# One DMA ring in a fixed order with 8-row tiles, in place of two rings with 6-row tiles, for silu(x1)*x2

## The chip, the cores and the metric

The kernel runs on one core of a Trainium2 chip. Times are device microseconds of a whole execution.

"Engine" means two things below. VectorE, ScalarE and SyncE are the core's instruction engines. A "DMA engine" is one of the 16 that move bytes. A "ring" is the queue of transfers that one issuing engine fills: SyncE's shows as q1, ScalarE's as q10.

## The reference

```python
batch, seq, dim = (32, 512, 2048)            # float32
x1, x2 = x[..., :1024], x[..., 1024:]
out = x1 * (1 / (1 + np.exp(-x1))) * x2      # [32, 512, 1024]
```

There are 16,384 rows: 134.2 MB in, 67.1 MB out, and little arithmetic for each byte.

## The kernel before

128 partitions each take a run of consecutive rows: tiles of 4 rows per partition, twenty times 6, and 4 again. Loads are issued by SyncE, stores by ScalarE, so the two directions sit in two rings.

```python
in_pool  = ctx.enter_context(tc.tile_pool(name="in_pool", bufs=2))
out_pool = ctx.enter_context(tc.tile_pool(name="out_pool", bufs=4))
# plan = [4] + [6]*20 + [4] rows per partition; KC = 2
for bi, (row0, K) in enumerate(plan):
    xv = x_flat[row0:row0 + P * K].rearrange("(p k) d -> p k d", k=K)
    ov = out_flat[row0:row0 + P * K].rearrange("(p k) d -> p k d", k=K)
    xt = in_pool.tile([P, KT, in_cols], dt, name="xt")
    nc.sync.dma_start(out=xt[:, :K, :], in_=xv)              # load, SyncE's ring
    ot = out_pool.tile([P, KT, half], dt, name="ot")
    for c in range(0, K, KC):
        ce = min(c + KC, K)
        nc.scalar.activation(out=ot[:, c:ce, :], in_=xt[:, c:ce, :half], func=Silu)
        nc.vector.tensor_mul(out=ot[:, c:ce, :], in0=ot[:, c:ce, :], in1=xt[:, c:ce, half:])
    nc.scalar.dma_start(out=ov, in_=ot[:, :K, :])            # store, ScalarE's ring
# (names shortened, asserts cut)
```

## Time and profile before

The time before is 474.58 us, the median of three runs (474.44 to 474.65).

| | before |
|---|---|
| span of the profile | 473.1 us |
| bytes moved | 201.35 MB, 426 GB/s over the span |
| DMA share and rate from 36 to 459 us | 1.00, 433 GB/s |
| VectorE, ScalarE busy | 30%, 25% |

The page of the kernel before: busy time of the two compute engines, the DMA row in 40 slices (tenths of the 16 DMA engines' time), and the two rings with packets, MB and share of the 16 engines' span.

```profile
span 473.1 us, 296 instructions
DVE 142.9 (30%) x64; ACT 118.9 (25%) x65; POOL 0.2 (0%) x4
DMA  8999999999999999999999999999999999999995
q1 hardware_dynamic: 3168, 134.22, 65.9%
q10 hardware_dynamic: 3168, 67.11, 33.0%
```

The DMA row is full until its last digit. The compute engines are idle most of the time and only wait for loads. The last digit, 5, is the one visible weakness. The windows view of the same kernel opens it up. Its columns are the stretch, its length, busy time of each engine with its instructions in brackets, the TensorE clock, the DMA share and GB/s.

```profile
core 0: us, DVE busy (x) ACT busy (x) POOL busy (x), PEclk, DMA share, GB/s
36.00:459.00 423.00, 130.55 (x59) 104.88 (x58) 0.00 (x0) 1.00 1.00 433
463.50:466.50 3.00, 2.22 (x2) 0.00 (x0) 0.00 (x0) 1.00 0.00 0
```

The timeline of the kernel before from 459 us on (start, length, engine, line, operation; in brackets the idle time before it and what ended that):

```profile
459.29 3.71 ACT L64 ACTIVATE ot<-xt 128x2048 f32<-128x2048 f32 x2 [10.47 <-DMA xt<-in_x_dram]
461.23 4.49 DVE L69 TENSOR_TENSOR ot<-ot,xt 128x2048 f32<-128x2048 f32 x2 [9.29 <-ACT ot L64]
465.76 0.34 ACTq L74 DMA_DIRECT2D out_dram<-ot  x1
```

The last load has landed at 459.3 us. Both chunks must be computed before the one store is issued at 465.8 us, and the other stores run out at about 463.5 us: 3.0 us in which no byte moves.

### The profile page before, as it was taken

The page shows a single profiled execution, that of the slowest core. Times are in us where ns is not written, and L with a number is a line of the kernel's source. Part 1 is how long each engine was busy: PE and PEld are TensorE (multiplying, and loading weights), DVE is VectorE, ACT ScalarE, POOL GpSimd, SP SyncE. Part 2 cuts the span into 40 slices and gives each one's busy share as a digit, 9 for nine tenths or more (in the row PEclk, how much of TensorE's full clock was granted, in tenths as well). Part 3 has the DMA queues.
Part 4 walks back from the last instruction along what each step waited for, and adds up shares of the span by engine and source line. Part 5 has one row for each costly group of instructions (what it writes and reads, how often), then busy time and mean ns, then how long its engine had stood idle before and what let it go on. Part 6 is the DMA issues. An engine that isn't in the chain of part 4 may idle for free.

```text
span 473.1 us, 296 instructions
## 1 busy us (share of the span) xinstructions
DVE 142.9 (30%) x64; ACT 118.9 (25%) x65; POOL 0.2 (0%) x4
## 2 busy tenths in 40 slices
DVE  0323505050514324050505142231505050513323
ACT  1340404041231404040413214040404042231411
POOL 0000000000000000000000000000000000000000
DMA  8999999999999999999999999999999999999995
GB/s 355 449 398 424 432 430 455 420 428 451 414 432 441 432 443 432 416 434 447 426 428 457 418 435 436 443 432 424 432 443 418 438 453 411 451 432 418 433 420 244
DMA packets 6338, 201.35 MB, mean 426 GB/s; under 512 B 704, under 2 KB 704, under 8 KB 704
## 3 DMA queue, kind: packets, MB, share of 16 engines
q1 hardware_dynamic: 3168, 134.22, 65.9%
q10 hardware_dynamic: 3168, 67.11, 33.0%
q14 instruction: 2, 0.02, 0.0%
HBM read 134.22 MB, written 67.11 MB: 426 GB/s over the span
## 4 chain that ended last, share of the span: by engine, by line
DMA 78%; DVE 14%; ACT 4%; issue 1%; DVEq 0%; SPq 0%; ACTq 0%
DMA xt<-in_x_dram 78%; DVE ot L69 14%; ACT ot L64 4%; DVEq L100 0%; SPq L59 0%; ACTq L64 0%
## 5 line engine op out<-in xcount | busy, mean ns | idle before, releaser
L69 DVE TENSOR_TENSOR ot<-ot,xt 128x2048 f32<-128x2048 f32 x64 | 142.9, 2287 | 322.8 <-ACT ot L64 322.8
L64 ACT ACTIVATE ot<-xt 128x2048 f32<-128x2048 f32 x64 | 117.6, 1899 | 343.4 <-DMA xt<-in_x_dram 343.4
L64 ACT ACT_TABLE_LOAD x1 | 1.3, 1283 | 0.7 <-PEq L89 0.7
L89 POOL MEMSET const-bfloat16-1.0<- 128x1 bf16 x1 | 0.1, 103 | 0.0
L89 POOL MEMSET const-uint8-127<- 128x1 uint8 x1 | 0.1, 103 | 0.0
L89 POOL MEMSET const-float32-1.0<- 128x1 f32 x1 | 0.1, 100 | 0.0
L89 POOL MEMSET const-float32-0.0<- 128x1 f32 x1 | 0.1, 99 | 0.2 <-issue 0.2
## 6 DMA issues: line engine op xcount, KB each, us to landing
xt<-in_x_dram SPq DMA_DIRECT2D x20, 6144.0 KB, 34.8
out_dram<-ot ACTq DMA_DIRECT2D x20, 3072.0 KB, 27.8
xt<-in_x_dram SPq DMA_DIRECT2D x2, 4096.0 KB, 20.7
out_dram<-ot ACTq DMA_DIRECT2D x2, 2048.0 KB, 15.4
```

The costliest lines, as they stand in the source:

```text
L64: nc.scalar.activation(out=ot[:, c:ce, :], in_=xt[:, c:ce, :half], func=mybir.ActivationFunctionType.Silu,)
L69: nc.vector.tensor_mul(out=ot[:, c:ce, :], in0=ot[:, c:ce, :], in1=xt[:, c:ce, half:],)
L89: nc = _bacc.Bacc("TRN2", target_bir_lowering=False, num_devices=1)
```

## The change

Its intent: fewer and longer runs in HBM (64 KiB loads, 32 KiB stores), a fixed order of load and store in one ring so that the two directions do not mix, store issues off ScalarE's queue, and a last store in four pieces so that the first bytes leave sooner.

```diff
-    K_MAIN = 6
-    K_EDGE = 4
+    K = 8
     KC = 2
-    out_pool = ctx.enter_context(tc.tile_pool(name="out_pool", bufs=4))
+    out_pool = ctx.enter_context(tc.tile_pool(name="out_pool", bufs=2))
     ... (plan of tiles cut)
+    def load(i):
+        xt = in_pool.tile([P, K, in_cols], dt, name="xt")
+        nc.sync.dma_start(out=xt, in_=xv[i])
+        loaded[i] = xt
+    load(0)
+    load(1)
+    for i in range(n_tiles):
+        xt = loaded.pop(i)
+        last = i == n_tiles - 1
     ... (activation and multiply by chunks of 2 rows, unchanged)
-        nc.scalar.dma_start(out=ov, in_=ot[:, :K, :])
+            if last:
+                nc.sync.dma_start(out=ov[i][:, c:ce, :], in_=ot[:, c:ce, :])
+        if not last:
+            nc.sync.dma_start(out=ov[i], in_=ot)
+        if i + 2 < n_tiles:
+            load(i + 2)
```

The ring then holds L0 L1 S0 L2 S1 L3 ... S13 L15 S14 and the four pieces of S15. Below, "L5" and "S5" are the load and the store of tile 5.

More of the change, by code (lines that the diff above doesn't have):

```diff
@@ L24 @@
     dt = x_flat.dtype
-    K_MAIN = 6
-    K_EDGE = 4
+    K = 8
     KC = 2
+    n_tiles = num_rows // (P * K)
+    assert n_tiles * P * K == num_rows
     in_pool = ctx.enter_context(tc.tile_pool(name="in_pool", bufs=2))
-    out_pool = ctx.enter_context(tc.tile_pool(name="out_pool", bufs=4))
-    rows_per_part_total = num_rows // P
-    rem = rows_per_part_total - 2 * K_EDGE
-    if rem > 0 and rem % K_MAIN == 0:
-        plan_k = [K_EDGE] + [K_MAIN] * (rem // K_MAIN) + [K_EDGE]
-    else:
-        plan_k = []
-        rem = rows_per_part_total
-        while rem > 0:
-            k = min(K_MAIN, rem)
-            plan_k.append(k)
-            rem -= k
-    plan = []
-    row = 0
-    for k in plan_k:
-        plan.append((row, k))
-        row += P * k
-    assert row == num_rows
-    KT = max(K_MAIN, K_EDGE)
-    for bi, (row0, K) in enumerate(plan):
-        xv = x_flat[row0:row0 + P * K].rearrange("(p k) d -> p k d", k=K)
-        ov = out_flat[row0:row0 + P * K].rearrange("(p k) d -> p k d", k=K)
-        xt = in_pool.tile([P, KT, in_cols], dt, name="xt")
-        nc.sync.dma_start(out=xt[:, :K, :], in_=xv)
-        ot = out_pool.tile([P, KT, half], dt, name="ot")
+    out_pool = ctx.enter_context(tc.tile_pool(name="out_pool", bufs=2))
+    xv = x_flat.rearrange("(n p k) d -> n p k d", p=P, k=K)
+    ov = out_flat.rearrange("(n p k) d -> n p k d", p=P, k=K)
+    loaded = {}
+    def load(i):
[7 more added lines that the diff above has]
+        last = i == n_tiles - 1
+        ot = out_pool.tile([P, K, half], dt, name="ot")
         for c in range(0, K, KC):
-            ce = min(c + KC, K)
+            ce = c + KC
             nc.scalar.activation(
```

## The prediction

In the text below, the 463 us are an estimate, worked out from the port ceiling that it cites.

> **What bounds the kernel now.** The 16 DMA engines. On the profile's page VectorE is busy 30% of the span and ScalarE 25%, while the DMA row reads 9 in nearly every slice. From 36 to 460 us the windows view gives a DMA share of 1.00 at 433 GB/s. The Trainium skill ("DMA: Bandwidth & Descriptors", Where 436 GB/s comes from) puts the port ceiling at 435 GB/s; the trace agrees within half a per cent. The job moves 201.3 MB whatever the tiling, at 435 GB/s 463 us of the 473.1 us span. About 10 us is to win.
>
> **Where those 10 us are** (the trace's packet records of before):
> - about 2.0 us at the start, before all engines carry data;
> - a hole at the end: packets run out at about 463.5 us and start again at 466.6 us (window 463 to 467: DMA share 0.18). The last load landed at 459.3 us; two activations and two multiplies must finish (465.7 us) before the one last store is issued. About 3.0 us;
> - about 1.5 us from the last data packet to the end;
> - a fixed cost per packet: 49,152 B take 1815 ns, 24,576 B 912 ns, so about 9 ns are fixed, the rest runs at 27.2 B/ns; 352 data packets per engine cost about 3.2 us;
> - about 1.8 us of slow first packets.
>
> **What the change does.**
> 1. Last store in four pieces, the store of tile 14 queued right behind the last load. Estimate from the trace: activation 1.9, multiply 2.29 us, so pieces are ready about 4.2, 6.5, 8.8 and 11.1 us after the last load lands, plus about 1.3 us issue. The store before them keeps the engines busy for 9.7 us, each piece 2.4 us. The last piece is ready before its turn (17 us), so the hole closes: -3.0 us, on the critical path.
> 2. Fewer, longer packets: 128 x 64 KiB, 120 x 32 KiB and 32 x 8 KiB per engine, 280 instead of 352: -0.65 us. If a 64 KiB run is cut in two, about +0.5 us instead.
> 3. One ring instead of two: nothing. Load-only (2 to 20 us) and store-only (459 to 463 us) stretches of before run packets at the same durations as the mixed ones; no gap shows between the first two loads. The queue must not run dry: compute of a tile takes about 11 us, the load still queued behind it 19.3 us, so the next store and load are issued in time though the one queue waits in order.
> 4. Store issues leave ScalarE (22 x 0.36 us): off the critical path.
>
> Sum: 474.6 - 3.0 - 0.6 = 471.0 us, 0.8% faster. Range 469.3 to 473.6. Faster by over 2%: 1%; within 2%: 94%; slower by over 2%: 5%.
>
> **What would show it right.** The DMA row full until the last slice, no hole before the last store; all data on one queue, about 5,040 packets (about 7,090 if 64 KiB runs are cut); steady rate about 433 GB/s; 64 KiB packets at about 2417 ns.
>
> **What would make it wrong.** Gaps at the 30 switches between store and load in one ring: this pattern is not in the trace of before; 0.3 us each would be +9 us, three times the gain. Or a 64 KiB stride between partitions in HBM that slows reads (packets above 2430 ns; 32 and 48 KiB show no such thing). Or the ring running dry, seen as DMA gaps ended by a VectorE wait on SP.

## The result, and the profile after

The changed kernel took 476.43 us (median of 4 runs, 475.81 to 476.81), against 474.55 us for the kernel before in the same rounds. The ratio is 1.0037, with a 95% interval of 1.0022 to 1.0051. A ratio is the mean time of one kernel's runs over that of the other's in the same rounds, so it is not quite the ratio of the medians. The change costs 0.4% instead of saving 0.8%. The predicted range was 469.3 to 473.6 us.

The page of the changed kernel:

```profile
span 474.4 us, 266 instructions
DVE 142.4 (30%) x64; ACT 118.2 (25%) x65; POOL 0.2 (0%) x4
DMA  8999999999999999999999999999999999989996
DMA packets 5042, 201.35 MB, mean 424 GB/s; under 512 B 560, under 2 KB 560, under 8 KB 560
q1 hardware_dynamic: 5040, 201.33, 98.8%
```

Much of what was predicted is there. One ring carries everything, with exactly 5,040 packets, so 64 KiB runs are not cut in two. The DMA row is full and shows no dry ring. The windows of the changed kernel:

```profile
core 0: us, DVE busy (x) ACT busy (x) POOL busy (x), PEclk, DMA share, GB/s
36.00:448.00 412.00, 124.57 (x56) 102.33 (x56) 0.00 (x0) 1.00 1.00 432
459.50:469.20 9.70, 5.43 (x3) 1.90 (x2) 0.00 (x0) 1.00 1.01 420
469.60:473.10 3.50, 0.00 (x0) 0.00 (x0) 0.00 (x0) 1.00 0.19 80
```

The last line is the surprise. From 469.6 to 473.1 us the DMA engines are not idle and not busy, but at 0.19: three or four of the sixteen still work and the others have finished. And the timeline of the changed kernel at its end:

```profile
454.09 7.31 ACT L56 ACTIVATE ot<-xt 128x2048 f32<-128x2048 f32 x4 [21.64 <-DMA xt<-in_x_dram]
456.03 8.90 DVE L61 TENSOR_TENSOR ot<-ot,xt 128x2048 f32<-128x2048 f32 x4 [20.05 <-ACT ot L56]
458.35 6.94 SPq L67 DMA_DIRECT2D out_dram<-ot  x4
```

The last load lands at 454.0 us.

### Looking at single DMA engines

The views above average over the 16 DMA engines, so I went to the trace's packet records (start, duration, bytes, ring of each packet). They do not name their engine. But a busy engine starts a packet within a few ns of the end of the one before, so the records can be sorted into 16 sequences. Where two engines' packets end together, sequences can be swapped by mistake; a jump by a whole packet is such an artefact or can be one, and I do not use it. A tile's load is eight packets per engine. "Lag" is the end of the eighth packet on an engine minus the median of the 16.

The lag in ns of the four latest engines at every second load of the changed kernel, worked out from these records (the other twelve stay within about 0.5 us of the median):

```
load          L1    L3    L5    L7    L9   L11   L13   L15
engine a     418   635  1587  2372  3360  3996  4365  4845
engine b     486   786  2087  2746  3662  3865  4415  4702
engine c     240   264   462  1248  2041  2701  3393  3719
engine d     137   205   249   557  1309  1839  2533  3005
```

In the kernel before, about five engines are late too, by 0.8 to 1.6 us after L2. But they keep that lag to the ns over most of the execution. In the changed kernel lag grows, tile by tile.

Where does it grow? A 65,536 B packet takes 2418 ns nearly always (predicted: 2417). From 60 us on, 45 of the 224 load packets that are directly followed by a store are stretched by more than 60 ns, up to 988 ns. Of the 1,505 that are followed by another load, 2 are. Of 208 store packets followed by a load, none is. So the loss is at one place: the last packet of a load before a store, on engines that are late already. Of the 45, 40 are on the four engines of the table; the other five are stretched by at most 0.13 us. In this kernel it is the last packet alone: on these engines 11 second-last load packets also ran for more than 1 us after the median engine had gone over to its store, and none is stretched.

How this becomes time: 12 engines run out of packets at 469.2 to 469.3 us and the last one at 473.2 us, 3.9 us. The lag also delays the landing of the last load, because a load has landed when its last DMA engine is done. The median engine finishes it at 448.8 us, the last at 453.7 us. So the first piece of the last store is issued late, at 458.35 us, and twelve engines idle 0.2 to 1.1 us at 459 us before it. The 3.9 us and about 1 us together account for the 4.9 us from the span that the prediction amounts to (473.1 less 3.6, 469.5 us) to the measured 474.4 us.

### The profile page after: what moved, and what is told of

The parts are those of the page before. It is cut to its first block, busy times and chain, and to the rows that moved or that the text cites. A ratio compares the mean times of both kernels' runs of the same rounds, so it can differ in the third digit from the quotient of the medians.

```text
span 474.4 us, 266 instructions
## 1 busy us (share of the span) xinstructions
DVE 142.4 (30%) x64; ACT 118.2 (25%) x65; POOL 0.2 (0%) x4
## 3 DMA queue, kind: packets, MB, share of 16 engines
q1 hardware_dynamic: 5040, 201.33, 98.8%
## 4 chain that ended last, share of the span: by engine, by line
DMA 79%; DVE 15%; ACT 3%; SPq 1%; DVEq 0%; issue 0%; ACTq 0%
DMA xt<-in_x_dram 79%; DVE ot L61 15%; ACT ot L56 3%; SPq L69 1%; DVEq L97 0%; SPq L45 0%; ACTq L56 0%
```

## The experiments

Theory A: sharing one ring makes late DMA engines later at each switch from load to store, and the slowest engine sets the time. Rival B: 64 KiB packets, or their stride in HBM, do it. Fifteen kernels ran.

### 1. two_rings_k8: the change without its one ring

```diff
-                nc.sync.dma_start(out=ov[i][:, c:ce, :], in_=ot[:, c:ce, :])
+                nc.scalar.dma_start(out=ov[i][:, c:ce, :], in_=ot[:, c:ce, :])
-            nc.sync.dma_start(out=ov[i], in_=ot)
+            nc.scalar.dma_start(out=ov[i], in_=ot)
```

> The changed kernel with its stores moved back to ScalarE's ring; tiles of 8 rows and the four-piece last store stay. Theory A (on one ring, the last load packet before a store is stretched on the engines that run late, 0.1 to 1.0 us each time, and their lag grows tile by tile to 4.8 us): lag stays constant as in the kernel before (0 to 1.6 us), no stretched packets after the first store, time about 471 to 472 us. Rival B (64 KiB load packets or their stride cause it): lag grows as in the changed kernel, about 476 us.

Measured: 471.95 us (471.85 to 472.20, 4 runs), ratio to the kernel before 0.9941 (0.9926 to 0.9956). The latest engine's lag is 0.48 us at L1, still 0.48 us at L10, and at most 0.75 us at L15. Of 1,504 load packets followed by a store packet, 2 are stretched. The page of this kernel, then its windows:

```profile
span 470.1 us, 267 instructions
q1 hardware_dynamic: 2304, 134.22, 66.3%
q10 hardware_dynamic: 2736, 67.11, 33.1%
```

```profile
36.00:448.00 412.00, 124.55 (x56) 102.32 (x56) 0.00 (x0) 1.00 1.01 434
464.50:466.00 1.50, 0.78 (x1) 0.00 (x0) 0.00 (x0) 1.00 0.52 218
468.70:470.10 1.40, 0.00 (x0) 0.00 (x0) 0.00 (x0) 1.00 0.00 0
```

The same 5,040 packets, on two rings, end together: all 16 engines stop between 468.7 and 468.8 us. Only the ring differs from the changed kernel, so the one ring costs 4.5 us (476.43 less 471.95). B falls.

### 2. one_ring_k6: the one ring with the old tiles

```diff
-        nc.scalar.dma_start(out=ov, in_=ot[:, :K, :])
+            if last:
+                nc.sync.dma_start(out=ov[:, c:ce, :], in_=ot[:, c:ce, :])
+        if not last:
+            nc.sync.dma_start(out=ov, in_=ot[:, :K, :])
+        if i + 2 < len(plan):
+            load(i + 2)
 # (cut: load(i) on SyncE and out_pool bufs=2, as in the changed kernel)
```

> The tiles of the kernel before (4, 20 x 6, 4 rows) with everything on one ring in the fixed order and the last store in two pieces. Theory A: last load packets (48 KiB) before a store are stretched on late engines and the lag grows over 21 switches to 3 us or more; time 474 to 478 us. Rival B: no growth, about 471 to 472 us.

Measured: 475.74 us (475.01 to 476.29), ratio 1.0015 (0.9997 to 1.0033). Four engines' lag grows, from 0.3 to 0.5 us at L2 to 3.0, 4.3, 4.4 and 4.7 us at the last load. From 60 us on 33 of the 288 last load packets are stretched. So A holds with 48 KiB packets too. The last engine stops at 473.1 us, as in the changed kernel.

### 3. one_ring_k8_halves: shorter load packets on the one ring

```diff
-        nc.sync.dma_start(out=xt, in_=xv[i])
+        nc.sync.dma_start(out=xt[:, :4, :], in_=xv[i][:, :4, :])
+        nc.sync.dma_start(out=xt[:, 4:, :], in_=xv[i][:, 4:, :])
```

> The changed kernel with each load cut in two DMAs of 32 KiB packets; ring, order and tile stay, 15 switches from load to store. Theory A: growth of the lag stays, 474 to 478 us, with stretched 32 KiB packets only at the end of the second half. Rival B (64 KiB packets): no growth, about 471.5 to 472.5 us.

Measured: 475.34 us (474.91 to 475.69), ratio 1.0011 (0.9996 to 1.0026). Fewer engines are hit in the profiled run: the last stops 2.9 us after the median one, the second last 1.4 us after it. The stretched packets stand at the end of second halves, which a store follows (16 of 224); at the end of first halves, which another load follows, I find none. So the 64 KiB packet is not the cause. Whether shorter packets soften the effect, one profiled run does not show.

### 4. tail_pieces: the cut last store alone

```diff
+        last = bi == len(plan) - 1
+        step = 1 if last else KC
-        for c in range(0, K, KC):
-            ce = min(c + KC, K)
+        for c in range(0, K, step):
+            ce = min(c + step, K)
-        nc.scalar.dma_start(out=ov, in_=ot[:, :K, :])
+            if last:
+                nc.scalar.dma_start(out=ov[:, c:ce, :], in_=ot[:, c:ce, :])
+        if not last:
+            nc.scalar.dma_start(out=ov, in_=ot[:, :K, :])
```

> The kernel before with its last tile computed and stored one row at a time (four pieces on ScalarE's ring), nothing else changed. If the 3.0 us hole before the last store is what a cut last store removes: about 471.5 us, 3 us under the kernel before, and no hole between the last two stores. If the cut gives nothing by itself: 474.5 us.

Measured: 471.91 us (471.87 to 472.10), ratio 0.9940 (0.9925 to 0.9955): 2.7 us saved where 3.0 were expected. In the windows of this kernel the stretch that was empty before is full:

```profile
463.50:466.50 3.00, 1.23 (x1) 1.06 (x1) 0.00 (x0) 1.00 1.02 419
```

### 5. Two attempts at the last microsecond on two rings

two_rings_k8 keeps a hole of 1 us near 465 us. In its timeline ScalarE issues three pieces, waiting for each multiply, before it runs its last activation at 461 us:

```profile
451.99 5.51 ACT L56 ACTIVATE ot<-xt 128x2048 f32<-128x2048 f32 x3 [21.54 <-DMA xt<-in_x_dram]
456.26 4.74 ACTq L67 DMA_DIRECT2D out_dram<-ot  x3
461.05 1.91 ACT L56 ACTIVATE ot<-xt 128x2048 f32<-128x2048 f32 x1 [3.55 <-DVE ot L61]
465.31 0.34 ACTq L67 DMA_DIRECT2D out_dram<-ot  x1
```

two_rings_tail_sp issues the four pieces from SyncE, which has no loads left by then:

```diff
 # against the changed kernel
-            nc.sync.dma_start(out=ov[i], in_=ot)
+            nc.scalar.dma_start(out=ov[i], in_=ot)
```

> Two rings, 8 rows a tile; whole-tile stores from ScalarE, the four pieces of the last store from SyncE, so that ScalarE does not wait for a multiply before its next activation. If the 1 us left of the hole in two_rings_k8 (DMA idle at about 464 to 466 us) comes from ScalarE's queue waiting to issue piece 3: hole gone, about 471.0 us, 1 us under two_rings_k8. If the pieces are late for another reason: 472.0 us.

Measured: 471.78 us (471.75 to 471.83), ratio 0.9941 (0.9925 to 0.9958). The hole closed, the time did not follow: from 457.6 us on, when the first of these pieces starts, 11 packets of 8 KiB took 0.7 to 1.1 us more than their usual 309 ns. This was the first store on SyncE's ring. The first store in every kernel shows such a cost near 25 to 40 us (see the list at the end).

two_rings_late_issue leaves the pieces with ScalarE, each issued one chunk later in the program:

```diff
 # against two_rings_k8
-            if last:
-                nc.scalar.dma_start(out=ov[i][:, c:ce, :], in_=ot[:, c:ce, :])
+            if last and c >= KC:
+                nc.scalar.dma_start(out=ov[i][:, c - KC:c, :], in_=ot[:, c - KC:c, :])
+        if last:
+            nc.scalar.dma_start(out=ov[i][:, K - KC:, :], in_=ot[:, K - KC:, :])
```

> two_rings_k8 with each piece of the last store issued by ScalarE one chunk later in its program, so that its queue does not wait for a multiply before the next activation. The last piece should be issued about 11 us after the last load's landing in place of 13 us; the 1 us of DMA idle near 465 us goes: about 471.0 us. If it stays at 471.9 us, the hole has another cause.

Measured: 472.19 us (471.74 to 472.42, 5 runs), ratio 0.9947 (0.9934 to 0.9961). The last piece is now issued at 463.5 instead of 465.3 us and there is no hole. Fifteen engines stop at 467.6 to 468.1 us, 0.6 to 1.1 us earlier than in two_rings_k8. The sixteenth stops at 469.0 us; it had lost 0.9 us at 311 us (below). So the expected 1 us is there for most engines, and one late engine takes it away. Three variants on two rings, and the kernel before with a cut last store, all end at 471.8 to 472.2 us. None beats the others clearly; all beat the kernel before by about 0.6%.

### 6. What in the switch does it: three looks

Reading M1: a late engine is slowed because the others are all in their store phase together. Reading M2: each switch in a ring costs the late engine by itself.

one_ring_alternate cuts the store of tile i and the load of tile i+2 in halves and alternates them:

```diff
-        if not last:
-            nc.sync.dma_start(out=ov[i], in_=ot)
         if i + 2 < n_tiles:
-            load(i + 2)
+            xn = in_pool.tile([P, K, in_cols], dt, name="xt")
+            loaded[i + 2] = xn
+        H = K // 2
+        for h in range(0, K, H):
+            if not last:
+                nc.sync.dma_start(out=ov[i][:, h:h + H, :], in_=ot[:, h:h + H, :])
+            if i + 2 < n_tiles:
+                nc.sync.dma_start(out=xn[:, h:h + H, :], in_=xv[i + 2][:, h:h + H, :])
```

> One ring as in the changed kernel, but store of tile i and load of tile i+2 are each cut in two DMAs and alternate: half store, half load, half store, half load; twice as many switches from load to store. 16 packets more per engine and tile cost about 9 ns each, 2.3 us over 15 tiles. Reading M2 (each switch on a ring costs the late engine by itself): stretched packets at the end of both halves, the lag of the last engine grows at least as much as in the changed kernel, 5 us or more, time 478 to 483 us. Reading M1 (a late engine is slowed because the others are all in their store phase together): shorter phases, same or less growth, time 473 to 478 us.

Measured: 475.43 us (475.35 to 475.62), ratio 1.0018 (1.0003 to 1.0033). With twice the switches, 20 of 432 last load packets are stretched instead of 45 of 224. The last engine stops 3.1 us after the median one, where it was 3.9. M2, a cost of every switch, expected 478 to 483 us and falls; M1's 473 to 478 us holds. The counts compare only roughly, because in this run three engines end late, by 1.4 to 3.1 us, where it was four. And M1 is not the whole of it: the second-last packets counted above also ran beside the others' stores and were not stretched. With the 32 KiB load packets of this run it is no longer the last packet alone either: six second- or third-last ones on the late engines are stretched by 0.3 to 1.0 us.

one_ring_small_stores has a wrong result; it stores only one row of eight:

```diff
-            nc.sync.dma_start(out=ov[i], in_=ot)
+            nc.sync.dma_start(out=ov[i][:, 0:1, :], in_=ot[:, 0:1, :])
```

> WRONG RESULT ON PURPOSE: the changed kernel storing only the first row (4 KiB) of each partition's 8 in tiles 0 to 14, so that a store phase lasts about 1.3 us instead of 9.7; 15 switches stay. About 350 us. M2 (the switch itself): last load packets are stretched on late engines as before and the lag grows by 3 us or more. M1 (the others' long store phase): little or no stretching, growth under 1 us.

Measured: 350.39 us (one look). Not one of 224 last load packets is stretched after the first store. But no engine was later than 0.3 us at L2 in this run, so it did not yet separate a short store phase from a lack of late engines.

one_ring_labelled was to tell which DMA engines are the late ones:

```diff
+    for n in range(1, 16):
+        w = 32 + 8 * n
+        nc.sync.dma_start(out=lab[:n, off:off + w], in_=x_flat[:n, off:off + w])
+        off += w
     load(0)
     load(1)
```

> The changed kernel behind 15 tiny loads of 1 to 15 partitions, each of its own size, so that packets of these sizes mark which of the 16 DMA engines a sequence of packets belongs to. Costs some 5 to 15 us at the start, no more is read from its time. Theory A expects the lag to grow on the engines that are late after the first tile; if the same engines are always late by their place in hardware they stand together by number, if by chance they are scattered.

This failed. Between such tiny packets the engines idle, and packets can no longer be chained to sequences, so the marks could not be followed. Its 480.28 us (one look) hold about 5 us of these loads; one engine's lag again grew, from 0.1 us at L1 to 2.7 us at L9. Which engines are late stays open.

### 7. Making engines late on purpose

Five small loads of 4 partitions between the first two tile loads give four engines five more packets of 8 KiB, which also mark them.

```diff
     load(0)
+    for n in range(5):
+        nc.sync.dma_start(out=lab[4*n:4*n+4], in_=xv[0][4*n:4*n+4, 0:1, :])
     load(1)
```

> The changed kernel with five extra loads of 4 partitions (one 8 KiB packet each on the same four DMA engines, about 0.31 us each) between the first two tile loads: these four engines are made about 1.5 us late, and carry 8 KiB packets early in the trace that mark them. If lateness is what gets a last load packet before a store stretched on one ring: these four lag engines, and above all these, show stretched packets at most switches and their lag grows to 4 us or more by the last tile. If it is chance or other engines' place in hardware: their lag stays about 1.5 us and other engines grow. Time 476 to 479 us.

> The same five extra loads in two_rings_k8. Theory A: the four engines stay about 1.5 us late from the first tile to the last, no stretched packets, 472.5 to 474 us. If lateness itself grows on any ring: lag over 3 us at the end.

> One ring, every tile's store issued as four DMAs of 2 rows (8 KiB packets) one after the other, so that the store phase stays 9.7 us long but its first packet is a quarter; 24 packets more per engine and tile at 9 ns are 3.2 us. If the length of the others' store phase counts: lag grows as in the changed kernel, stretched last load packets on late engines. If the size of the store packet that follows counts: little stretching, growth under 1 us, as with the small stores.

The third kernel is the changed one with every store issued as four:

```diff
-            nc.sync.dma_start(out=ov[i], in_=ot)
+            for c in range(0, K, KC):
+                nc.sync.dma_start(out=ov[i][:, c:c + KC, :], in_=ot[:, c:c + KC, :])
```

Measured on one ring: 476.33 us (one look). Four sequences carry the five extra packets. They are the late ones: 1.2, 1.8, 2.0 and 2.5 us at L1, and 5.3, 4.1, 4.2 and 4.4 us at L15. A fifth, unmarked one grew from 0.3 to 2.5 us. The other eleven end within 0.4 us of the median. This is what lateness as the trigger predicts. It does not exclude that these four engines are prone to it by their place: every run with imposed lag uses the same five loads, and none makes four other engines late.

Measured on two rings: 476.95 us (one look), where 472.5 to 474 us was expected. The lags are 1.4, 1.5, 3.4 and 3.5 us at L1 and the same within a few ns at L7. After that, three of them go up by single jumps, to 4.5 us at most, in two cases beside a gap of 0.3 us (at 288 and 316 us; see the instruction queue in the last list). So lag does not grow by itself on two rings, as A said. But the two engines became 3.5 us late, not 1.5, and the expectation had left out what lag does at the end: the last load lands at 457.2 us instead of 452.0 us, as the timeline of that kernel shows, and all engines then idle 0.8 to 4.6 us at 462 us. With engines this late from the start, two rings are no faster than one (476.95 against 476.33 us, one look each): what costs time is the lag, however it arises.

```profile
457.20 5.51 ACT L60 ACTIVATE ot<-xt 128x2048 f32<-128x2048 f32 x3 [21.75 <-DMA xt<-in_x_dram]
```

Measured with stores in pieces: 480.07 us (479.29 and 480.85), ratio 1.0114. Lag grows as in the changed kernel, to 3.1 to 5.6 us on four engines; 105 of 226 last load packets are stretched. So it is not the size of the store packet that follows. This run is also the slowest of the whole-result kernels timed in rounds. 3.2 us of it were expected from the extra packets.

### 8. Three controls with imposed lag

> WRONG RESULT ON PURPOSE: one_ring_imposed_lag storing only the first row (4 KiB) of 8 per partition in tiles 0 to 14. If a long store phase of the other engines is needed: the four marked engines stay about 1.5 to 2.5 us late, with no growth over 0.5 us. If the earlier run without growth only lacked late engines: their lag grows to 4 us or more here too.

> WRONG RESULT ON PURPOSE: the same with 4 of 8 rows stored (store phase about 4.9 us, packets of 16 KiB). If the amount of store traffic counts: growth between that of the small stores and that of whole stores, some 1 to 2 us, or a lower ceiling (whole stores: about 4 to 5 us, half a store phase; here 2.5 us). If only the presence of large stores counts: growth as with whole stores.

> WRONG RESULT ON PURPOSE: one_ring_imposed_lag in which each store of tiles 0 to 14 is replaced by a load of the same size (32 KiB per partition) into the output tile, same place in the ring. If writes to HBM by the other engines stretch a late engine's last load packet: no stretched packets, lag flat at 1.5 to 2.5 us. If any change of DMA in the ring does it: growth as in one_ring_imposed_lag.

All three give wrong results and have one_ring_imposed_lag's five small loads; the store lines are:

```diff
-            nc.sync.dma_start(out=ov[i], in_=ot)
+            nc.sync.dma_start(out=ov[i][:, 0:1, :], in_=ot[:, 0:1, :])   # lag_small_stores
+            nc.sync.dma_start(out=ov[i][:, 0:4, :], in_=ot[:, 0:4, :])   # lag_half_stores
+            nc.sync.dma_start(                                           # lag_loads_for_stores
+                out=ot.rearrange("p (a b) d -> p a (b d)", b=2),
+                in_=xv[i][:, 0:4, :])
```

The lag of the four marked engines in us, and stretched last load packets after 60 us:

| kernel | time, us | lag at L1 | lag at L7 | stretched |
|---|---|---|---|---|
| one_ring_imposed_lag (whole stores) | 476.33 | 1.2, 1.8, 2.0, 2.5 | 3.0, 3.2, 3.4, 4.0 | 31 of 224 |
| lag_half_stores | 403.28 | 1.8, 2.2, 2.2, 2.4 | 1.8, 2.2, 2.2, 2.4 | 15 of 224, none before L8 |
| lag_small_stores | 352.74 | 1.4, 1.9, 2.0, 2.5 | 1.4, 1.9, 2.0, 2.5 | 0 of 225 |
| lag_loads_for_stores | 474.62 | about 1.2, 1.5, 2.1, 2.4 | about the same | 0 of 224 |

With loads in place of the stores, the same bytes, packets, order and lateness, not one packet is stretched (some sequences are swapped in that trace, so its lags are approximate). So it takes stores. This control replaced the late engine's own stores together with those of the others, and a store both reads SBUF and writes HBM; which of these matters is not shown.

The amount of storing seems to count: with small stores nothing is stretched, and with half stores the four marked engines stayed where they were to L7. Ten of the 15 stretched packets of lag_half_stores stand at one switch, L8 to S7, at 209 to 212 us, on punctual engines too, which I cannot explain. How the amount acts is open as well. The last load packet of an engine that is 2.2 us late ends 2.2 us after the others began to store, when a phase of 4.9 us is no more over than one of 9.7 us.

One limit: these three controls ran on another chip (9) than one_ring_imposed_lag (15), and no run with whole stores on one ring was made on chip 9.

## Why the prediction was wrong, point by point

- **What bounds the kernel: right.** The DMA engines at 432 to 434 GB/s in the steady part of the three kernels shown above. The Trainium skill ("DMA: Bandwidth & Descriptors", Where 436 GB/s comes from) gives 435 GB/s; the traces agree.
- **Step 1, the hole at the end: right in mechanism, nearly in size.** Alone, cutting the last store saved 2.7 us (tail_pieces) where 3.0 were predicted. In the changed kernel part of the hole came back, up to 1.1 us on twelve engines, because the last load lands late.
- **Step 2, packets: right in its parts.** 5,040 packets, 2418 ns. The predicted 0.65 us is visible on the median engine (its last packet ends at 467.8 us in two_rings_late_issue and 468.3 us in tail_pieces, both without a hole), but not in the time, which follows the last engine.
- **Step 3, "One ring instead of two: nothing": this step failed.** It measured 4.5 us (476.43 against 471.95 us). I had looked at packets that go load to load or store to store on one ring, found no gap, and took the 16 engines as one. The runs showed that the load to store switch on one ring stretches the last load packet of late engines while the others store, and that the time is that of the last engine. The list of dangers named the switches as not seen in the trace of before, but expected gaps on all engines at all 30; it came as longer packets on about four engines, at the 15 switches of one direction.
- **Running dry: right.** Stores and loads were issued 9 us and more before their turn (S0 at 33.6 us for 42.6 us, S3 at 112.8 us for 129.8 us).
- **Step 4, store issues off ScalarE: right,** worth nothing in the steady part.
- **The range** was built around the steps' sizes and left little room for the step marked "nothing", although the text itself called that pattern unseen.

What stays open is the mechanism below this: why, of 64 KiB packets, only the last of a load is stretched on a late engine, how the amount of storing acts, why lag levels off at 4 to 5 us, about half a store phase of 9.7 us, and which engines are late.

## What to carry to other kernels

When a kernel is bound by DMA, try loads and stores on two rings before a strict order on one. Here reads and writes then mixed packet by packet and lag did not grow, while the one ring cost 1%. Read DMA per engine, not as an average of 16. A low share has more than one meaning: 0.19 at the end of the changed kernel was a few late engines, 0.18 from 463 to 467 us in the kernel before was a hole on all of them. Both a load's landing and the end of the kernel were set here by the last engine. At a full DMA row, look for the win in the tail: cutting the last store in four on the old kernel was a few lines and worth 0.6%.

## What the Trainium skill lacked or had wrong

- "DMA: Bandwidth & Descriptors", Issuing engines are not separate DMA queues, says that starting DMAs on several engines will "only save the time on the sequencer it takes to initiate the DMA". Here the issuing engine of the stores made 4.5 us of 472 (476.43 against 471.95 us), with the same packets; the measurement decides.
- The same page, Queues, rings and completion order, says that each DMA engine goes round robin between its rings by packet. The traces agree: on two rings load and store packets alternate (1,488 of 1,792 store packets are followed by a load packet in two_rings_k8). On two rings late engines did not fall further behind (0.48 us at L1 and at L10); no page has that.
- No page has it that on one ring a load's last packet before a store is stretched, by up to 1.0 us, mostly on engines that are late (45 of 224 in the changed kernel; with imposed lag 31 of 224, against 0 of 224 with loads in place of the stores).
- The same page, SWDGE vs HWDGE vs iDMA, gives a packet as at most 4096 B preferably, in its account of the path from GpSimd (SWDGE). The loads here are issued by SyncE, and on that ring the trace records packets of 65,536 B, 2418 ns each, with a fixed part of about 9 ns. Whether the trace's packet is what the page calls one is not shown, but on two rings the DMA engines alternate between the rings by just these packets.
- No page has the cost of the first store: the packets around it take longer by about 1.0 us per engine in the kernel before, about 1.5 us in the changed one, and about 0.7 to 1.1 us again when a second ring has its first store late in two_rings_tail_sp.
- The same page, Queues, rings and completion order, names row 14 as runtime-internal (refill); no page gives the time that this takes from a busy DMA engine. Two packets of 8 KiB on the instruction queue (q14) in the middle of the execution (at 310.2 and 310.6 us in two_rings_late_issue) are followed by one or two engines being 0.4 to 1.1 us later in the kernels on two rings, and nothing takes that back.
